# Modulation vectors by multiply-and-sum on VectorE over a transposed matrix, in place of matmuls, copies and transposes

## Chip, cores and metric
The kernel runs on one core of one Trainium2 chip. The metric is the device time of one execution in microseconds (us); shown is the median of three runs. TensorE is called PE, VectorE DVE, ScalarE ACT, GpSimd POOL and SyncE SP, as in the profile. PEld is PE's weight load.

## What is computed
Two residual blocks follow one another over 256 tokens of 1024 channels, each with two layers. In both, each layer first derives a modulation (shift, scale and gate, 1024 numbers each) from a conditioning vector; block 2 does so for the stream x and for a context stream, from two vectors and with the same matrix. Everything is float32.

```python
def hybrid_layer(x, c_silu, ...):                      # block 1, two layers
    mod = c_silu @ w_ada + b_ada                       # [1, 1024] x [1024, 3072]
    shift, scale, gate = jnp.split(mod, 3, axis=-1)
    u = rms_norm(x, norm_g) * (1 + scale[:, None]) + shift[:, None]
    z = u @ w_in
    # three attentions (a: top-k index selection, b: sliding window, c: stick-breaking) on parts of z
    merged = (jax.nn.sigmoid(ma) * (ya @ w_br_a) + jax.nn.sigmoid(mb) * (yb @ w_br_b)
              + jax.nn.sigmoid(mc) * (yc @ w_br_c))
    return x + gate[:, None] * (merged @ w_out)

def mixer_layer(x, cx, c, c_ctx, ...):                 # block 2, two layers
    shift, scale, gate = jnp.split(jax.nn.silu(c) @ w_ada + b_ada, 3, axis=-1)
    shift_c, scale_c, gate_c = jnp.split(jax.nn.silu(c_ctx) @ w_ada + b_ada, 3, axis=-1)
    h = x * (1.0 + scale[:, None]) + shift[:, None]
    hc = cx * (1.0 + scale_c) + shift_c
    # h @ w_in, hc @ w_in, four mixers (A recurrent, B and D attention, C differential attention)
    x_new = layer_norm(alpha * x + gate[:, None] * (y @ w_out), ln_g, ln_b)
```

## The kernel before
The streams are kept channel-major, 128 partitions by 8 channel groups by 256 tokens (`xT`). Every large product is made of three, since each operand is split into a high and a low part: a weight tile of 256 columns arrives as two half tiles of 512 KB (`wr`, issued by SP), ACT copies out the high part `wh` (L111), DVE subtracts for the low part `wl` (L112), and PE runs high by high, low by high and high by low (L104, `proj_tok` and `proj_ch`). There are three `wr` buffers and four each of `wh` and `wl`. The input u of a layer is split likewise: DVE makes `af` (L439), ACT `uh`, DVE `ul` (L441). In block 2 the same tiles are `hxh`, `hxl` for the stream x and `hch`, `hcl` for the context.

A norm (`rstd_row`, L321) sums squares over channels on PE with a matrix of ones, turns them into a column pair `rc` (L329 on DVE, a power on POOL), spreads them with a diagonal `dg` (L333) on PE again and copies the row to `rstd` (L336). Until `af`, `uh` and `ul` of the first channel groups are there, PE has no product of the next layer to run.

The modulation is made by jobs (`ada`, L271). A job makes 256 of the 3072 numbers: it loads two half tiles of w_ada (into `wsp`, which takes idle tags, or into `wr`), runs 8 products with the 32 columns `cs` of conditioning vectors as the small operand (L288; the trace counts two instructions each), copies the sum to `adas` on ACT (L290), transposes it twice on PE (L293, shown under L108), and ends with a reduction `adar` (L295) and a multiply-and-add `mod` (L296) on DVE. Each layer has 12 jobs in each block, 48 in all; one job serves both of block 2's vectors. Eight run at the start, since the first layer's shift and scale are needed at once. The others wait in a list `bg`; `after_tile` (L235) adds `rate` to `due` behind each weight tile and runs a job for each whole number reached. The rates are 0.32 in block 1's first layer, 0.2 in its second and 0.8 in block 2's first. `flush(4)` behind each layer of block 1 runs what is left but four, and `fill` (L241) runs four of these at the norm between block 1's layers and two at the norm into block 2, with weights in tags that are idle there.

The order in each engine's queue isn't that of the code: the tile framework schedules the program once, by its own estimates of times, and each engine then works through its queue in order. So a waiting instruction holds back all behind it on its engine, on SP's queue of transfers too.

## Time and profile before
| | |
|---|---|
| median of 3 runs | 1383.55 us (1381.17 to 1384.69) |
| profiled execution, span | 1377.4 us |
| time outside the span, against the median | 6.2 us |
| PE busy | 1330.4 us (97%) |
| PEld busy | 1164.2 us (85%) |
| DVE busy | 844.3 us (61%) |
| ACT busy | 655.1 us (48%) |
| POOL busy | 25.4 us (2%) |

The profile was taken from one execution. Its span runs from the first to the last instruction that it shows; the median was taken over other executions and holds 6.2 us more. Busy times of matmuls are those of pipelined instructions, each shown longer than the distance to the next. Durations on DVE overlap a little too where its queue is full: the next instruction starts before the last has ended. Block 1's first layer runs to about 372 us, its second to about 717, block 2's first to about 1088, its second to the end.

### The profile page before, as it was taken

The page shows a single profiled execution, that of the slowest core. Times are in us where ns is not written, and L with a number is a line of the kernel's source. Part 1 is how long each engine was busy: PE and PEld are TensorE (multiplying, and loading weights), DVE is VectorE, ACT ScalarE, POOL GpSimd, SP SyncE. Part 2 cuts the span into 40 slices and gives each one's busy share as a digit, 9 for nine tenths or more (in the row PEclk, how much of TensorE's full clock was granted, in tenths as well). Part 3 has the DMA queues.
Part 4 walks back from the last instruction along what each step waited for, and adds up shares of the span by engine and source line. Part 5 has one row for each costly group of instructions (what it writes and reads, how often), then busy time and mean ns, then how long its engine had stood idle before and what let it go on. Part 6 is the DMA issues. An engine that isn't in the chain of part 4 may idle for free.

```text
span 1377.4 us, 27990 instructions
## 1 busy us (share of the span) xinstructions
PE 1330.4 (97%) x11682; PEld 1164.2 (85%) x11682; DVE 844.3 (61%) x1744; ACT 655.1 (48%) x1178; POOL 25.4 (2%) x23
## 2 busy tenths in 40 slices
PE   5999999999999999999998999999999998999996
PEld 2998987899889898789998989977877788997774
DVE  3795454655559544565576366756577777775764
ACT  3455555544444545654443233346455546534652
POOL 0000000000000000000000000000000000000000
PEclk9899999999999999999999999999999999999998
DMA  9754746568746474547764442322143355522111
GB/s 330 216 151 131 232 142 190 158 204 266 227 124 184 123 212 141 153 138 220 211 214 153 135 142 63 109 93 77 52 139 118 107 154 159 175 81 62 62 62 46
DMA packets 199214, 205.07 MB, mean 149 GB/s; under 512 B 8368, under 2 KB 197424, under 8 KB 198448
## 3 DMA queue, kind: packets, MB, share of 16 engines
q1 hardware_dynamic: 199088, 203.28, 48.3%
q8 instruction: 92, 1.51, 0.4%
q14 instruction: 34, 0.28, 0.1%
HBM read 199.06 MB, written 4.19 MB: 148 GB/s over the span
## 4 chain that ended last, share of the span: by engine, by line
PE 82%; DMA 6%; DVE 4%; issue 4%; ACT 2%; SPq 1%; POOL 0%; POOLq 0%; ACTq 0%; DVEq 0%
PE ps L104 77%; PE ps L108 5%; DMA wr<-w_in 4%; DMA wsp<-w_ada 2%; DVE wl L112 2%; ACT wh L111 1%; SPq L219 1%; DMA wr<-w_out 0%; DMA cT<-ctx 0%; DVE KTc L829 0%; DVE af L439 0%; ACT Xx L1305 0%; ACT pe L402 0%; ACT L566 0%; DVE QTc L827 0%
## 5 line engine op out<-in xcount | busy, mean ns | idle before, releaser
L112 DVE TENSOR_TENSOR wl<-wr,wh 128x1024 fp32r<-128x1024 f32 (+1 forms) x270 | 328.4, 1217 | 258.3 <-ACT wh L111 255.8
L111 ACT ACTIVATE wh<-wr 128x1024 fp32r<-128x1024 f32 (+1 forms) x270 | 284.6, 1055 | 378.2 <-PE ps L104 255.2
L104 PE MATMUL ps<-uh,wh 128*128 128x256 f32 x704 | 202.2, 287 | 2.4 <-ACT thm L566 2.4
L104 PE MATMUL ps<-ul,wh 128*128 128x256 f32 x704 | 200.9, 285 | 0.0
L104 PE MATMUL ps<-uh,wl 128*128 128x256 f32 x704 | 200.8, 285 | 0.0
L104 PEld LDWEIGHTS ps<-uh,wh 128*128 128x128 f32 x704 | 132.7, 188 | 8.2 <-issue 4.4
L104 PEld LDWEIGHTS ps<-ul,wh 128*128 128x128 f32 x704 | 132.8, 189 | 1.9 <-issue 1.7
L104 PEld LDWEIGHTS ps<-uh,wl 128*128 128x128 f32 x704 | 132.7, 188 | 1.9 <-issue 1.6
L104 PE MATMUL ps<-wh,uh 128*128 128x256 f32 (+1 forms) x416 | 120.2, 291 | 2.0 <-ACT uh L440 1.2
L104 PE MATMUL ps<-wl,uh 128*128 128x256 f32 (+1 forms) x416 | 119.9, 289 | 1.0 <-DVE wl L112 1.0
L104 PE MATMUL ps<-wh,ul 128*128 128x256 f32 (+1 forms) x416 | 120.0, 289 | 0.1
L402 ACT ACTIVATE pe<-ps,nm 128x512 f32<-128x512 f32 (+2 forms) x160 | 84.9, 539 | 54.4 <-DVE nm L397 41.1
L397 DVE TENSOR_REDUCE nm<-ps 128x1 f32<-128x512 f32 (+2 forms) x104 | 71.1, 687 | 42.2 <-PE ps L104 42.0
L104 PEld LDWEIGHTS ps<-wh,uh 128*128 128x128 f32 x416 | 81.2, 196 | 4.1 <-ACT uh L440 1.4
L104 PEld LDWEIGHTS ps<-wl,uh 128*128 128x128 f32 x416 | 81.3, 196 | 1.8 <-DVE wl L112 1.3
L104 PEld LDWEIGHTS ps<-wh,ul 128*128 128x128 f32 x416 | 81.5, 196 | 1.2 <-DVE ul L441 0.9
L104 PE MATMUL ps<-wh,hxh 128*128 128x256 f32 x256 | 72.4, 283 | 0.0
L104 PE MATMUL ps<-wh,hxl 128*128 128x256 f32 x256 | 72.1, 281 | 0.0
L104 PE MATMUL ps<-wl,hxh 128*128 128x256 f32 x256 | 72.0, 281 | 0.0
L104 PE MATMUL ps<-hxh,wh 128*128 128x256 f32 x224 | 64.9, 294 | 4.2 <-ACT hxh L440 4.2
L104 PE MATMUL ps<-hxl,wh 128*128 128x256 f32 x224 | 64.6, 290 | 2.7 <-DVE hxl L441 2.7
L104 PE MATMUL ps<-hxh,wl 128*128 128x256 f32 x224 | 64.6, 290 | 0.6 <-DVE wl L112 0.6
(351 smaller groups left out, 3150.7 us busy)
## 6 DMA issues: line engine op xcount, KB each, us to landing
wr<-w_in SPq DMA_DIRECT2D x204, 512.0 KB, 4.0
wsp<-w_ada SPq DMA_DIRECT2D x68, 512.0 KB, 5.7
wr<-w_out SPq DMA_DIRECT2D x40, 512.0 KB, 3.7
wr<-w_ada SPq DMA_DIRECT2D x28, 512.0 KB, 3.9
wr<-w_br_a SPq DMA_DIRECT2D x8, 512.0 KB, 3.9
wr<-w_br_c SPq DMA_DIRECT2D x8, 512.0 KB, 4.6
wr<-w_br_b SPq DMA_DIRECT2D x8, 512.0 KB, 4.6
Xx<-resx SPq DMA_DIRECT2D x2, 1024.0 KB, 4.7
```

Of the source, the lines that this page charges most:

```text
L104: self.nc.tensor.matmul(o, l, r, start=start, stop=stop, skip_group_check=True)
L108: self.nc.tensor.transpose(o, i, self.ident[:n, :n])
L111: self.nc.scalar.activation(h, x, AF.Copy)
L112: self.nc.vector.tensor_tensor(l, x, h, op=OP.subtract)
L219: self.nc.sync.dma_start(out=w[:, :, :n], in_=ap[k0 * 128:k0 * 128 + 512, c0:c0 + n].rearrange("(k p) n -> p k n", p=128))
L397: nc.vector.tensor_reduce(nmx, p, axis=AX.X, op=OP.max, negate=True)
L402: nc.scalar.activation(e[:, j, :], p[:, j, :], AF.Exp, bias=nm[:, h:h + 1], accum_out=ss[:, h:h + 1])
```

## The change
The two matrices w_ada and w_ada_2 are handed over transposed, so that a chunk holds 128 outputs on the partitions and the 1024 inputs along a row of 4 KB. A conditioning vector is loaded once onto all 128 partitions (`cond_row`), and twice its silu is made in place (tanh on ACT, one multiply-and-add on DVE, in two halves). A job is now two chunks; for each and for each vector, one DVE instruction multiplies chunk and vector, sums along the row, halves, adds the bias and leaves a column of `mod`. The products themselves go to `junk`, a single bfloat16 buffer that nobody reads. In the program it is two entries on DVE, the sum and the read of its accumulator: 144 pairs. The column operand `cs`, the copies and the transposes go, and both `fill` with them; the rates are 0.5, 0.3 and 0.8. A setting makes the framework's scratch space for transfers smaller, which frees on-chip memory for the new buffers. On PE the program has 8070 rows before and 7964 now, on DVE 1399 and 1604, on ACT 755 and 707, on SP 153 and 162.

```diff
-    def fill(self, n, tags):
-        """waiting jobs for a stretch in which the streams' chain leaves TensorE idle; their weights go to idle tags"""
-        keep, self.spare = self.spare, tags
-        for _ in range(min(n, len(self.bg))):
-            self.bg.popleft()()
-        self.spare = keep
...
+    def cond_row(self, v):
+        nc = self.nc
+        r = self.const.tile([128, 1024], F32, name="crow", tag=f"crow{v // 2}")
+        src = self.I["cond"][1024 * v:1024 * v + 1024]
+        nc.sync.dma_start(out=r, in_=bass.AP(tensor=src.tensor, offset=src.offset, ap=[[0, 128], [1, 1024]]))
+        for h in (slice(0, 512), slice(512, 1024)):
+            th = self.W("cth", [128, 512], tag="th")
+            nc.scalar.activation(th, r[:, h], AF.Tanh, scale=0.5)
+            nc.vector.scalar_tensor_tensor(r[:, h], th, 1.0, r[:, h], op0=OP.add, op1=OP.mult)
+        return r
...
         def load(n):
-            return [self.raw(wa, k, n * 256, 256, True) for k in (0, 4)]
+            ws = []
+            for c in (2 * n, 2 * n + 1):
+                if self.spare:
+                    w = self.K("wsp", [128, 1024], tag=self.spare[self.nspare % len(self.spare)])
+                    self.nspare += 1
+                else:
+                    w = self.wr.tile([128, 1024], F32, name="wr", tag="wr")
+                nc.sync.dma_start(out=w, in_=wa[:, c])
+                ws.append(w)
+            return ws
 
         def job(n, ws=None):
-            p = self.P(self.pj, [128, 512])
-            for k in range(8):
-                g = 32 * (k % 4)
-                self.mm(p[g:g + 32, :256], self.cs[:, k, :], ws[k // 4][:, k % 4, :], start=k < 4, stop=k >= 4)
-            sb = self.W("adas", [128, 256], tag="score")
-            nc.scalar.activation(sb, p[:, :256], AF.Copy)
-            pc = self.P(self.tr, [128, 2, 4, 32])
-            for j in range(2):
-                self.T(pc[:, j].rearrange("p g v -> p (g v)"), sb[:, 128 * j:128 * j + 128])
-            r = self.W("adar", [128, 2, nv])
-            nc.vector.tensor_reduce(r, pc[:, :, :, v0:v0 + nv].rearrange("p j g v -> p j v g"), axis=AX.X, op=OP.add)
...
+            for c, w in enumerate(ws or load(n)):
+                c += 2 * n
+                for v, r in enumerate(crow):
+                    junk = self.const.tile([128, 1024], BF, name="junk", tag="junk")
+                    nc.vector.tensor_tensor_reduce(out=junk, in0=w, in1=r, scale=0.5, scalar=bias[:, c:c + 1],
+                                                   op0=OP.mult, op1=OP.add, accum_out=mod[:, c, v:v + 1])
...
-        if l == 1:
-            self.fill(4, ["a4", "a5", "a6", "g1", "g2", "g3", "t3a", "t3b"])
...
-        N.rate = 0.32 if l == 0 else 0.2
+        N.rate = 0.5 if l == 0 else 0.3
...
-    N.fill(2, ["a7", "g1", "g2", "g3"])
...
+    for n in ("w_ada", "w_ada_2"):
+        a[n] = np.ascontiguousarray(inputs[n].reshape(2, 1024, 24, 128).transpose(0, 3, 2, 1))
+    a["cond"] = np.concatenate([inputs[n].reshape(-1) for n in ("c", "c_2", "c_ctx_2")])
```

The queue of DVE at the start, where the first layer's input is made. The names: `g1` and `mod10` come from the modulation, `rstd` from the norm, `c_identb` is a constant. Before:

```order
L449 SCALAR_TENSOR_TENSOR g1_322<-mod10_106,cols_87 128x2
L439 SCALAR_TENSOR_TENSOR af_353<-xT_117,g1_322,rstd_320 128x256
L439 SCALAR_TENSOR_TENSOR af_357<-xT_117,g1_322,rstd_320 128x256
L112 TENSOR_TENSOR wl_364<-wr_279,wh_363 128x1024
L441 SCALAR_TENSOR_TENSOR ul_328<-af_353,mod10_106,uh_327 128x256
L112 TENSOR_TENSOR wl_368<-wr_281,wh_367 128x1024
L441 SCALAR_TENSOR_TENSOR ul_328<-af_357,mod10_106,uh_327 128x256
L112 TENSOR_TENSOR wl_434<-pre_283,wh_433 128x1024
L112 TENSOR_TENSOR wl_438<-pre_283,wh_437 128x1024
L167 CAST c_identb_577<-cb_571 128x128
```

And now, the last parts of the same input:

```order
L112 TENSOR_TENSOR wl_261<-wr_176,wh_260 128x1024
L440 SCALAR_TENSOR_TENSOR ul_225<-af_242,mod10_107,uh_224 128x256
L440 SCALAR_TENSOR_TENSOR ul_225<-af_246,mod10_107,uh_224 128x256
L296 ISA junk_174,mod10_107<-wsp_170,crow_99,cols_87 128x1024
L296 ISA mod10_107 128x1
L112 TENSOR_TENSOR wl_265<-wr_178,wh_264 128x1024
L112 TENSOR_TENSOR wl_331<-pre_180,wh_330 128x1024
L448 SCALAR_TENSOR_TENSOR g1_219<-mod10_107,cols_87 128x2
L112 TENSOR_TENSOR wl_335<-pre_180,wh_334 128x1024
L438 SCALAR_TENSOR_TENSOR af_250<-xT_118,g1_219,rstd_217 128x256
L438 SCALAR_TENSOR_TENSOR af_254<-xT_118,g1_219,rstd_217 128x256
L158 CAST c_identb_474<-cb_468 128x128
```

The sums stand where the small reductions stood, and the last `ul` moved to a place further down than the rows shown, behind four `wl` and behind constants that wait for transfers (`csg`, `pr`).

The queue of DVE at the norm between block 1's two layers. Before:

```order
L336 COPY rstd_4206<-ps_4196 128x256
L295 TENSOR_REDUCE adar_4328<-ps_4325 128x2
L439 SCALAR_TENSOR_TENSOR af_4215<-xT_117,g1_4208,rstd_4206 128x256
L439 SCALAR_TENSOR_TENSOR af_4219<-xT_117,g1_4208,rstd_4206 128x256
L296 SCALAR_TENSOR_TENSOR mod11_290<-adar_4328,cols_87 128x2
L581 TENSOR_SCALAR g4_7749<-mod11_290 128x8
L441 SCALAR_TENSOR_TENSOR ul_4214<-af_4215,mod11_290,uh_4213 128x256
L441 SCALAR_TENSOR_TENSOR ul_4214<-af_4219,mod11_290,uh_4213 128x256
L439 SCALAR_TENSOR_TENSOR af_4223<-xT_117,g1_4208,rstd_4206 128x256
L439 SCALAR_TENSOR_TENSOR af_4227<-xT_117,g1_4208,rstd_4206 128x256
L441 SCALAR_TENSOR_TENSOR ul_4214<-af_4223,mod11_290,uh_4213 128x256
L441 SCALAR_TENSOR_TENSOR ul_4214<-af_4227,mod11_290,uh_4213 128x256
```

And now (`mod20_3965` is the modulation of block 2's first layer, `crow_3949` and `crow_3957` its two vectors; `mod11` is that of the layer whose input is made):

```order
L335 COPY rstd_3995<-ps_3985 128x256
L296 ISA junk_5471,mod20_3965<-wsp_5463,crow_3957,cols_87 128x1024
L296 ISA mod20_3965 128x1
L438 SCALAR_TENSOR_TENSOR af_4004<-xT_118,g1_3997,rstd_3995 128x256
L438 SCALAR_TENSOR_TENSOR af_4008<-xT_118,g1_3997,rstd_3995 128x256
L296 ISA junk_5800,mod20_3965<-wsp_5796,crow_3949,cols_87 128x1024
L296 ISA mod20_3965 128x1
L703 COPY mc_7712<-mod20_3965 128x8
L703 COPY mc_7792<-mod20_3965 128x8
L440 SCALAR_TENSOR_TENSOR ul_4003<-af_4004,mod11_187,uh_4002 128x256
```

Sums for the block behind the next layer moved in between the steps that make u.

SP's queue of transfers at the same place, among the second layer's first weights (the rows with 68 columns are the narrow tile of the index weights). Before:

```order
L219 DMA wr_4413<-w_in 128x4x256
L219 DMA wr_4479<-w_in 128x4x68
L219 DMA wsp_4310<-w_ada 128x4x256
L219 DMA wr_4485<-w_in 128x4x68
L219 DMA wsp_4312<-w_ada 128x4x256
L219 DMA wr_4635<-w_in 128x4x256
L219 DMA wsp_4976<-w_ada_2 128x4x256
L219 DMA wsp_4978<-w_ada_2 128x4x256
L219 DMA wr_4641<-w_in 128x4x256
```

And now:

```order
L210 DMA wr_4190<-w_in 128x4x68
L210 DMA wr_4340<-w_in 128x4x256
L287 DMA wsp_5463<-w_ada_2 128x1024
L287 DMA wsp_5796<-w_ada_2 128x1024
L287 DMA wsp_5798<-w_ada_2 128x1024
L287 DMA wsp_6273<-w_ada_2 128x1024
L287 DMA wsp_6275<-w_ada_2 128x1024
L287 DMA wsp_6471<-w_ada_2 128x1024
L287 DMA wsp_6473<-w_ada_2 128x1024
L287 DMA wsp_6674<-w_ada_2 128x1024
L210 DMA wr_4346<-w_in 128x4x256
```

Eight chunks moved into one row ahead of the next weights; they use two tags, `t3a` and `t3b`.

## Rows read from the trace of the kernel before
**Rows 1.** The page: busy times of the engines, and the ended-last chain by line.
```profile
PE 1330.4 (97%) x11682; PEld 1164.2 (85%) x11682; DVE 844.3 (61%) x1744; ACT 655.1 (48%) x1178; POOL 25.4 (2%) x23
PE ps L104 77%; PE ps L108 5%; DMA wr<-w_in 4%; DMA wsp<-w_ada 2%; DVE wl L112 2%; ACT wh L111 1%; SPq L219 1%; DMA wr<-w_out 0%; DMA cT<-ctx 0%; DVE KTc L829 0%; DVE af L439 0%; ACT Xx L1305 0%; ACT pe L402 0%; ACT L566 0%; DVE QTc L827 0%
```
**Rows 2.** Windows: stretch, length, busy time (instructions) by engine, granted clock, DMA share, GB/s.
```profile
34.00:97.00 63.00, 61.73 (x482) 59.92 (x483) 51.35 (x127) 29.59 (x53) 0.00 (x0) 0.92 0.64 191
372.80:433.80 61.00, 58.09 (x481) 52.35 (x472) 42.17 (x100) 25.41 (x41) 0.70 (x1) 0.94 0.53 151
732.00:1088.00 356.00, 351.13 (x3482) 299.19 (x3482) 218.17 (x513) 155.19 (x332) 13.26 (x9) 1.00 0.34 105
```
**Rows 3.** Windows of `cs` alone (one row: PE, PEld, ACT), then of `adas`.
```profile
732.00:1088.00 356.00, 17.82 (x214) 6.62 (x214) 0.00 (x0) 0.75 (x2) 1.00 0.34 105
...
34.00:365.00 331.00, 3.87 (x20) 2.39 (x20) 3.80 (x10) 0.98 0.63 189
365.00:384.00 19.00, 2.57 (x12) 1.24 (x12) 2.29 (x6) 1.00 0.76 237
384.00:717.00 333.00, 3.10 (x16) 1.94 (x16) 3.03 (x8) 0.99 0.57 172
717.00:732.00 15.00, 0.85 (x4) 0.49 (x4) 1.02 (x3) 0.96 0.43 137
732.00:1088.00 356.00, 5.46 (x28) 3.40 (x28) 5.04 (x14) 1.00 0.34 105
```
**Rows 4.** Timeline of PE: start, duration, engine, line, operation, out<-in, shapes, count.
```profile
437.38 1.07 PE L104 MATMUL ps<-wsp,cs 128*32 128x256 f32 x16
438.38 0.60 PE L104 MATMUL ps<-akT,aqT 64*128 64x128 f32 x3
...
156.81 0.39 PE L108 MATMUL ps<-ident,adas 128*128 128x128 f32 x2
156.95 0.36 PE L104 MATMUL ps<-uh,wl 128*128 128x256 f32 x1
```
**Rows 5.** Groups of DVE by form: busy us, mean ns, idle before and releasers.
```profile
L112 DVE TENSOR_TENSOR wl<-wr,wh 128x1024 fp32r<-128x1024 f32 x268 | 327.6, 1223 | 255.6 <-ACT wh L111 253.2 <-ACT pe L402 0.8 <-PE ps L104 0.2
L933 DVE SCALAR_TENSOR_TENSOR pe<-pe,dc 128x512 f32<-128x512 f32 x16 | 12.0, 750 | 0.5
L439 DVE SCALAR_TENSOR_TENSOR af<-xT,g,rstd 128x256 f32<-128x256 f32 x16 | 7.0, 478 | 0.1
L608 DVE RECIPROCAL rec<-ss 128x1 f32<-128x1 f32 x32 | 5.1, 159 | 5.9 <-ACT pe L402 5.6
```
**Rows 6.** Timeline of DVE at the start, where the first input is finished.
```profile
34.80 1.22 DVE L112 TENSOR_TENSOR wl<-wr,wh 128x1024 fp32r<-128x1024 f32 x1
35.94 0.47 DVE L441 SCALAR_TENSOR_TENSOR ul<-af,mod,uh 128x256 fp32r<-128x256 f32 x1
...
37.47 0.47 DVE L441 SCALAR_TENSOR_TENSOR ul<-af,mod,uh 128x256 fp32r<-128x256 f32 x1
```
**Rows 7.** Windows of the start: the columns as in rows 2.
```profile
8.00:12.00 4.00, 3.10 (x22) 0.69 (x18) 0.33 (x2) 0.65 (x2) 0.00 (x0) 1.00 1.04 397
12.00:34.00 22.00, 15.13 (x132) 6.05 (x132) 8.64 (x34) 8.59 (x19) 0.70 (x1) 0.93 1.10 349
```
**Rows 8.** The ended-last chain in order of time, at the norm: start, us, what.
```profile
372.92 6.08 DMA wsp<-w_ada
```
**Rows 9.** Timeline of DVE at the same norm and behind it.
```profile
371.96 0.87 DVE L587 SCALAR_TENSOR_TENSOR xT<-ps,g,xT 128x256 f32<-128x256 f32 x2
...
388.74 0.88 DVE L441 SCALAR_TENSOR_TENSOR ul<-af,mod,uh 128x256 fp32r<-128x256 f32 x2 [0.18 <-ACT uh L440]
...
431.01 1.23 DVE L112 TENSOR_TENSOR wl<-wr,wh 128x1024 fp32r<-128x1024 f32 x1 [0.19 <-ACT wh L111]
```
**Rows 10.** The page, DMA issues: count, KB each, median us from issue to landing.
```profile
wsp<-w_ada SPq DMA_DIRECT2D x68, 512.0 KB, 5.7
```
**Rows 11.** Timeline of PE at the norm into block 2; idle before in brackets.
```profile
729.87 0.38 PE L104 MATMUL ps<-hxh,wh 128*128 128x256 f32 x1 [3.99 <-ACT hxh L440]
```

More of the change, by code (lines that the diff above doesn't have):

```diff
@@ L122, in load_consts @@
         self.mhalf = C.tile([128, 8], F32, name="mhalf")
-        self.cs = C.tile([128, 8, 32], F32, name="cs")
-        nc.vector.memset(self.cs, 0.0)
-        th = self.W("cth", [128, 24], tag="af")
-        nc.scalar.activation(th, cols[:, :24], AF.Tanh, scale=0.5)
-        for j in range(3):
-            o = 8 * j
-            nc.vector.scalar_tensor_tensor(self.cs[:, :, j], th[:, o:o + 8], 1.0, cols[:, o:o + 8],
-                                           op0=OP.add, op1=OP.mult)
         nc.vector.memset(self.sel4, 0.0)
@@ L271, in ada @@
     def ada(self, l, blk):
         nc = self.nc
-        nv = 1 if blk == 1 else 2
+        vs = (0,) if blk == 1 else (1, 2)
         wa = self.I["w_ada" if blk == 1 else "w_ada_2"][l]
-        v0 = blk - 1
-        mod = self.const.tile([128, 24, nv], F32, name=f"mod{blk}{l}")
-        def load(n):
-            return [self.raw(wa, k, n * 256, 256, True) for k in (0, 4)]
-        def job(n, ws=None):
-            ws = ws or load(n)
-            bias = self.colB[:, 48 * (blk - 1) + 24 * l:48 * (blk - 1) + 24 * l + 24]
-            p = self.P(self.pj, [128, 512])
-            for k in range(8):
-                g = 32 * (k % 4)
-                self.mm(p[g:g + 32, :256], self.cs[:, k, :], ws[k // 4][:, k % 4, :], start=k < 4, stop=k >= 4)
-            sb = self.W("adas", [128, 256], tag="score")
-            nc.scalar.activation(sb, p[:, :256], AF.Copy)
-            pc = self.P(self.tr, [128, 2, 4, 32])
-            for j in range(2):
-                self.T(pc[:, j].rearrange("p g v -> p (g v)"), sb[:, 128 * j:128 * j + 128])
-            r = self.W("adar", [128, 2, nv])
-            nc.vector.tensor_reduce(r, pc[:, :, :, v0:v0 + nv].rearrange("p j g v -> p j v g"), axis=AX.X, op=OP.add)
-            nc.vector.scalar_tensor_tensor(mod[:, 2 * n:2 * n + 2, :], r, 0.5,
-                                           bias[:, 2 * n:2 * n + 2][:, :, None].to_broadcast([128, 2, nv]),
-                                           op0=OP.mult, op1=OP.add)
@@ new lines, in ada @@
+        if l == 0:
+            self.crow = [self.cond_row(v) for v in vs]
+        crow = self.crow
+        mod = self.const.tile([128, 24, len(vs)], F32, name=f"mod{blk}{l}")
+        bias = self.colB[:, 48 * (blk - 1) + 24 * l:48 * (blk - 1) + 24 * l + 24]
+        def load(n):
+            ws = []
[8 more added lines that the diff above has]
+            return ws
@@ L1319, in _arrays @@
     a["cols"] = np.ascontiguousarray(np.concatenate(
-        [col(n) for n in ("c", "c_2", "c_ctx_2", "b_ada", "b_ada_2", "final_g", "norm_g", "ln_g_2", "ln_b_2")]
+        [col(n) for n in ("b_ada", "b_ada_2", "final_g", "norm_g", "ln_g_2", "ln_b_2")]
         + [twice(n) for n in ("hg_norm_g_2", "df_subln_g_2")] + [col("hg_lb_logits_2")], 1))
+    for n in ("w_ada", "w_ada_2"):
+        a[n] = np.ascontiguousarray(inputs[n].reshape(2, 1024, 24, 128).transpose(0, 3, 2, 1))
+    a["cond"] = np.concatenate([inputs[n].reshape(-1) for n in ("c", "c_2", "c_ctx_2")])
     a["rows"] = np.concatenate([inputs[n].reshape(-1) for n in (
```

6 lines of the change are left out of this document (3 added, 3 removed).

## Prediction
> **What bounds the kernel now.** I read the page's busy times first, then the chain that ended last, then the stretches one by one. TensorE (PE) is busy 1330.4 us of a span of 1377.4, and its products are 77% of the chain; VectorE (DVE) is busy 844.3 us, 61% [rows 1]. So the kernel is bound by PE almost everywhere, and a us that leaves PE's queue in a PE-bound stretch is a us off the end, as long as DVE still delivers the low weight halves `wl` in time. That average hides the places where DVE is already nearly full: 51.4 us of the 63 us behind the first product, and 42.2 of the 61 us behind the norm between block 1's two layers, while in block 2's first layer it has 138 us free of 356 [rows 2]. The change takes work from the engine that sets the end and gives about three times as much to DVE, so the question is where DVE has the room.
>
> **What leaves PE.** A job is 8 products (16 instructions) over `cs` and two transposes of `adas`. By the transposes, two to a job, there are 10 jobs from 34 to 365 us, 6 in the norm's gap, 8 from 384 to 717, 2 at the norm into block 2 and 14 behind it [rows 3]; the other 8 of the 48 are done in the first 34 us. Those 8 lie under the loading of the weights, the 6 lie in a gap in which PE has nothing else. That leaves 34 jobs on PE-bound stretches. One costs from start to start 1.00 us for the products and 0.14 for the transposes [rows 4], so 1.14 at the least; by busy time it is 17.82 / 14 + 5.46 / 14 = 1.66 with the overlap of pipelined ends counted in [rows 3]. I take 1.3, nearer to the start-to-start value: 34 x 1.3 = **-44 us** (-39 to -56). The ACT copy and DVE's two small operations of a job go too; they lie beside PE and bring nothing of their own.
>
> **What DVE gets.** There are 144 new multiply-and-sum instructions over 128 x 1024 (24 + 24 for block 1's two layers, 48 + 48 for block 2's, since there each chunk meets two vectors). The trace has none. From below: the subtraction that makes `wl`, 1024 elements from two SBUF inputs, takes 1223 ns, 1.14 from its start to the next instruction's when the queue is full [rows 5, 6]. From above: multiply-and-scale of 512 elements takes 750 ns, two of them 1.50, and a one-column operation behind it 159 ns, together 1.66 [rows 5]. I take 1.14 + 0.16 for the read of the sum + 0.1 for the wait on the one before (all write one `junk` buffer) = **1.4 us**; 144 x 1.4 = 202 us, which would put DVE near 1020 us of busy time. That still is under the span, so what matters is where they stand in DVE's queue, which works in order.
>
> [...]
>
> **The start (+5).** Before, weights land without a pause: 349 GB/s at a DMA share of 1.10, and 397 GB/s in the four us in which `xT`, with long rows, lands [rows 7]. The transposed matrix has rows of 4 KB instead of 1 KB, so its 8.4 MB could come in 21 us instead of 24; the broadcast vector of 0.5 MB costs 1.3 of it. Against that, 16 sums (22.4 us) now stand in DVE's queue between the steps that make the input u, where small reductions stood, and they can't begin before the vector's tanh. Behind the last chunk DVE still has to make parts of u, four `wl` and the constants; in the new order the last two `ul` stand behind constants that wait for transfers. Adding the rows in order puts the last `ul` near 44 to 45 us; before it stood at 37.47 [rows 6]. The first tile's products need it; they still had work of their own in hand at 37.47, so I take +5 of the 7 (0 to 10). In the 63 us behind it, DVE gets 16 sums; with the constants moved ahead the order adds up to 62.1 us against 62.5 elapsed, so DVE is full but not late: 0 (to +4).
>
> **The norm between block 1's layers (+17).** Before, the gap is stretched by the filled-in jobs themselves: a load of w_ada of 6.08 us stands on the chain there, and PE's queue holds the norm's sums behind its products [rows 8]. From the last `xT` (start 371.96) the last `ul` starts at 388.74; the `wl` of the twelfth full weight half behind it is made from 431.01 [rows 9], when PE is about to need it. The fill's removal shortens the gap by up to 4 us. But in the new order 17 sums of the next block's vectors stand from the last `xT` to the first narrow `wl`, in ones between each two pairs of `af` and `ul`, then four in a row: DVE was the idle engine there, so the scheduler put them there. The sum over DVE's queue from `xT` to that twelfth half is now 29 x 1.4 = 40.6 for the sums and 32.7 for the rest (the 42.2 of [rows 2] without overlaps and without the top-k selection, which now stands later), 73.3 in place of 60: PE is late by 13, the fill's removal counted in, since the sum begins at `xT`. By the same sum DVE has caught up some 108 us behind `xT`. On top, eight loads of chunks stand in SP's queue in one row and go to two buffers: a chunk can be fetched only when the sums over the last but one are done, and a load takes 5.7 us to land [rows 10] while DVE has 4.5 us of other work for each chunk. That gives 0 to 1.2 us for each of eight; I add 4 (0 to 9). Together **+17** (9 to 24). Who waits: `rc`, `dg`, `rstd` and `af` stand behind sums in the same queue, ACT's `uh` behind `af`, PE behind both; the weights of the next tiles wait in SP's queue behind the eight loads.
>
> **The norm into block 2 (+4).** PE's gap there is 3.99 us [rows 11], part filled by jobs. Sums now stand between `rc`, `dg`, `rstd` and `af`; about three of them at 1.4 us fall into the chain: +4 (2 to 6).
>
> **Block 2's first layer (+7).** 48 sums, 67 us, go into 138 us of free DVE time, and PE is ahead by the saved jobs. A stall comes where an operation that PE waits for finds a sum at work: 67 of 356 us are taken, a half sum (0.7 us) is left on average, and there are some 48 row maxima there: 48 x 0.19 x 0.7 = 6.4. I take +7 (3 to 18). Block 2's second layer has no jobs: 0.
>
> **The sum.** -44 + 5 + 0 + 17 + 4 + 7 = -11, so the span goes from 1377.4 to 1366. The median of the runs, 1383.55, stands 6.2 above the profiled span; with that, **1372**. The ends: -56 + 0 + 0 + 9 + 2 + 3 = -42 gives 1342, -39 + 10 + 4 + 24 + 6 + 18 = +23 gives 1407; all at one end at once is unlikely, and I take 1347 to 1403 for it.
>
> **Rivals.** A: DVE's room hides it all, because a sum is as cheap as `wl` and the order leaves the chain ahead. For it: 533 us of idle DVE time in all. Against it: the norm's queue, where even 1.14 a sum leaves 29 x 1.14 + 32.7 = 65.8 against 60. With -44, or -48 with the fill gone, it gives 1383.6 - 48 = **1336**.
> [...]
> C, the slower side: in block 2's first layer the softmax chains are one after another through DVE and ACT to PE, so a sum that stands ahead of a row maximum is not taken at random but put just where DVE is idle, which is where PE waits for it. If half of the 67 us is exposed, 34 instead of 7, the time is 1372 + 27 = **1399**. It turns slower than before from 7 + 12 = 19 us exposed, about 3 in 10 of the sums' time. For it: the same scheduler put sums into each gap of the norm. Against it: PE is 351 of 356 us busy there [rows 2], so it has little to wait for and tiles enough in hand.
> That the jobs don't leave PE can't be: the program's order has 106 instruction rows fewer on PE and no `adas`.
>
> **Chances.** Forecast 0.6, A 0.12, B 0.08, C 0.2. About 0.3% (4 us) is what a measurement can tell from no change: faster is under 1379.4, slower over 1387.7. Of the forecast's 0.6 I give 0.44 to faster, 0.09 to the same and 0.07 to slower; A is faster; B is slower; C is 0.03 same and 0.17 slower. Faster 0.56, same 0.12, slower 0.32. The range, which leaves out A below and B above (0.2 together) and takes in C, is 1346 to 1404.
>
> **What would show it.** PE's busy time should fall by some 75 us over the whole span and its idle time rise. [...] The last `ul` should start about 44 us at the start, and 27 us behind the last `xT` at the norm instead of 17. DVE should be busy 1000 to 1040 us, and PE's waits for `wl` and `ul` should be some 20 us longer. From 384 to 1088 no more than 7 us should be waits of PE for row maxima behind sums; over 20 means C. What would make me wrong most is the price of one sum: each 0.1 us moves the start and the norm by 3 to 6 us together.

## The result, and the profile after
The changed kernel takes 1395.62 us (median of four runs, 1390.64 to 1400.41) against 1382.36 for the kernel before (median of four, one run more than above): ratio 1.0095, interval 1.0066 to 1.0124. It is 13 us slower where 11 us faster was forecast. The profiled execution has a span of 1392.3 us (1377.4 before).

First the page of the changed kernel, the lines that answer to [rows 1], and the two groups of the new sums (busy us, mean ns of one, idle time before them and what ended it):

```profile
PE 1281.8 (92%) x10818; PEld 1147.5 (82%) x10818; DVE 1000.1 (72%) x1938; ACT 648.5 (47%) x1140; POOL 31.0 (2%) x23
PE ps L104 27%; DMA wr<-w_ada 4%; PE ps L108 3%; DVE junk L296 2%; DVE wl L112 1%; DVE nm L396 0%; POOL rec L347 0%; ACT wh L111 0%; DVE KTc L826 0%; ACT Xx L1301 0%; DVE Gx L428 0%; ACT pe L401 0%; DVE QTc L824 0%; DVE FTc L829 0%; DVE ssq L877 0%
...
L296 DVE CUSTOM_DVE_ANT_0 junk<-wsp,crow,cols 128x1024 bf16<-128x1024 f32 x96 | 123.0, 1281 | 12.8 <-DMA wsp<-w_ada 12.4
...
L296 DVE CUSTOM_DVE_ANT_0 junk<-wr,crow,cols 128x1024 bf16<-128x1024 f32 x48 | 61.6, 1283 | 29.6 <-DMA wr<-w_ada 29.0
```

PE lost 49 us of busy time and the span grew by 15: PE is idle 64 us more than before. DVE gained 156 us, less than the 202 of the forecast: a sum takes 1.28 us, 16 us of small operations are gone, and busy time counts the overlapped ends of back-to-back instructions once (DVE's groups add up to 1095 us here and 910 before, its busy time is 1000 and 844). New on the chain is `wr<-w_ada`: a load that only jobs wait for. (The chain could be followed back only to 753 us here, so its shares are not to be compared with those of before.) And DVE itself sits idle 41 us in front of sums whose chunk has not landed.

The windows (stretch, length, then busy time of PE, PEld, DVE, ACT and POOL, granted clock, DMA share, GB/s) show where DVE is full, first of the changed kernel, then two of the same stretches before:

```profile
31.00:165.00 134.00, 123.58 (x1005) 119.12 (x1006) 124.50 (x242) 58.07 (x86) 0.00 (x0) 0.99 0.94 308
379.00:440.00 61.00, 47.97 (x302) 43.67 (x303) 57.11 (x104) 17.17 (x28) 1.66 (x1) 0.72 0.66 196
735.00:935.00 200.00, 178.93 (x2129) 170.86 (x2130) 161.68 (x316) 63.73 (x108) 11.44 (x6) 0.96 0.43 129
...
379.00:440.00 61.00, 59.06 (x464) 54.85 (x465) 45.51 (x103) 26.11 (x39) 0.08 (x1) 0.94 0.50 142
735.00:935.00 200.00, 198.59 (x2347) 178.44 (x2347) 113.80 (x246) 71.84 (x132) 8.87 (x6) 1.00 0.36 111
```

DVE is busy 93% from the first product to 165 us; 94% in the norm between block 1's layers and behind it, where PE is busy 48 of 61 us and the granted clock is 0.72 (as a share of the highest; of the first 1365 windows of 1 us of this trace 1264 show 1.00 and 77 show 0.50); and 81% in the first 200 us of block 2. To these 161.7 us come the waits for chunks there, in the list of DVE's waits from 735 to 935 us (who waited for whom: us in total, times, longest):

```profile
DVE junk L296 <- DMA wr<-w_ada: 27.9, 17, 3.8
```

161.7 + 27.9 is 189.6 of 200 us: all but full. Then the sums' places over the span, 40 slices of 34.8 us, in tenths busy:

```profile
busy tenths in 40 slices 5233100000453300000012323210000000000000
```

They stand in three bunches: the start to 155 us, 353 to 476 us (across the norm between block 1's layers), 722 to 933 us. Between them DVE has no sum for 198 and 246 us. The rates of the jobs don't show in these places; the account for that is that the scheduler takes a job as soon as a buffer for its chunk is free (e12 below bears it out).

### The profile page after: what moved, and what is told of

The parts are those of the page before. It is cut to its first block, busy times and chain, and to the rows that moved or that the text cites. A ratio compares the mean times of both kernels' runs of the same rounds, so it can differ in the third digit from the quotient of the medians.

```text
span 1392.3 us, 26487 instructions
## 1 busy us (share of the span) xinstructions
PE 1281.8 (92%) x10818; PEld 1147.5 (82%) x10818; DVE 1000.1 (72%) x1938; ACT 648.5 (47%) x1140; POOL 31.0 (2%) x23
## 5 line engine op out<-in xcount | busy, mean ns | idle before, releaser
L104 PE MATMUL ps<-wh,uh 128*128 128x256 f32 (+1 forms) x416 | 123.9, 300 | 18.4 <-ACT wh L111 8.0
L296 DVE CUSTOM_DVE_ANT_0 junk<-wsp,crow,cols 128x1024 bf16<-128x1024 f32 x96 | 123.0, 1281 | 12.8 <-DMA wsp<-w_ada 12.4
L104 PE MATMUL ps<-wh,ul 128*128 128x256 f32 (+1 forms) x416 | 124.0, 299 | 3.8 <-DVE ul L440 3.8
L104 PEld LDWEIGHTS ps<-wh,uh 128*128 128x128 f32 x416 | 84.2, 204 | 22.1 <-ACT wh L111 8.7
L104 PEld LDWEIGHTS ps<-wh,ul 128*128 128x128 f32 x416 | 84.5, 203 | 6.7 <-DVE ul L440 5.4
L104 PEld LDWEIGHTS ps<-wl,uh 128*128 128x128 f32 x416 | 84.2, 203 | 5.4 <-DVE wl L112 5.0
L296 DVE CUSTOM_DVE_ANT_0 junk<-wr,crow,cols 128x1024 bf16<-128x1024 f32 x48 | 61.6, 1283 | 29.6 <-DMA wr<-w_ada 29.0
```

The lines of the kernel that those rows point to most:

```text
L104: self.nc.tensor.matmul(o, l, r, start=start, stop=stop, skip_group_check=True)
L296: nc.vector.tensor_tensor_reduce(out=junk, in0=w, in1=r, scale=0.5, scalar=bias[:, c:c + 1], op0=OP.mult, op1=OP.add, accum_out=mod[:, c, ...
```

## The experiments
All runs in one table: the span, and the stages of the profiled execution, in us. "Layer 1" ends with the last update of `xT` (counted from 0, the start included); a norm ends with the first product that uses the new input's low part (`ul`), or the first on `hxh` for block 2; block 2's first layer ends with the last gated update of the stream, `Xx<-ps,g,Xx`. What follows takes 265 to 268 us in every run. Stages with the same order of instructions differ by up to 3 us from run to run. More can come from the order alone: an edit elsewhere makes the scheduler place the first layer's instructions differently too, and in e1, whose edit is in block 2, that layer took 5.7 us longer.

| run | layer 1 | norm | layer 2 | norm | block 2, layer 1 | span |
|---|---|---|---|---|---|---|
| before | 372.8 | 10.9 | 333.5 | 12.7 | 381.0 | 1377.4 |
| changed | 379.3 | 14.0 | 332.6 | 13.7 | 387.4 | 1392.3 |
| e1 own buffers, block 2 | 385.0 | 12.4 | 332.9 | 9.9 | 383.7 | 1390.8 |
| e2 one chunk, block 2 | 380.4 | 13.8 | 343.6 | 11.9 | 368.6 | 1385.8 |
| e3 half sums, block 2 | 381.4 | 13.6 | 330.2 | 13.0 | 363.9 | 1367.7 |
| e4 no jobs | 351.4 | 7.5 | 326.9 | 9.9 | 363.7 | 1324.5 |
| e5 block 1 spread | 365.7 | 7.6 | 330.4 | 16.5 | 386.1 | 1372.3 |
| e6 layer 2 spread | 377.2 | 7.5 | 329.4 | 16.2 | 388.5 | 1384.0 |
| e7 four `wr` | 387.9 | 12.3 | 331.0 | 13.4 | 382.2 | 1392.3 |
| e8 all sums half | 371.6 | 10.1 | 335.8 | 13.8 | 371.0 | 1367.2 |
| e9 block 2's sums early, some | 368.8 | 12.0 | 358.2 | 17.2 | 359.8 | 1380.7 |
| e10 the same, all | 368.0 | 11.0 | 370.1 | 8.9 | 365.3 | 1389.0 |
| e11 before, new schedule | 387.1 | 7.5 | 340.4 | 11.0 | 386.0 | 1398.0 |
| e12 changed, old schedule | 373.0 | 13.2 | 338.4 | 14.8 | 386.3 | 1391.0 |
| e13 spread further | 384.4 | 8.7 | 331.0 | 18.0 | 366.0 | 1375.4 |
| e14 spread further yet | 385.1 | 10.6 | 333.6 | 17.8 | 361.7 | 1373.6 |
| e15 before, no fills | 375.4 | 7.4 | 332.3 | 32.5 | 391.0 | 1406.2 |
| e16 e14 with late vectors | 376.6 | 12.3 | 339.4 | 18.3 | 361.3 | 1373.4 |
| e17 e16 with fewer moved | 376.5 | 8.3 | 333.9 | 28.3 | 358.2 | 1370.4 |

### Block 2: buffers, loads, or the sums' own time (e1 to e4, e7)
Two theories on block 2 stood first: that chunks lack buffers, or that the sums' time in the queue costs.

e1, with tag g2 idle in block 2:

```diff
-    N.spare = None
+    N.spare = ["g2", "cw"]
     x, r = N.block2(0, R, H, mod, context_done)
```

> The changed kernel, but in block 2 the 24 chunks of w_ada go to two buffers of their own instead of the three `wr` buffers of the weights. Stage meant: block 2's first layer, 739.5 to 1126.9 us in the changed kernel (387.4 us, before 381.0). Theory T (buffer loop): a sum waits at the head of DVE's queue for a chunk whose load could start only when sums before it had freed a `wr` buffer, and the weights' splits wait behind it; then DVE's waits for w_ada fall from 29.0 us to under 10, the stage to 366-374 us, the run to about 1378. Rival W (work and order): the 48 sums' 65 us in an in-order queue do it, wherever the chunks lie; then the stage stays at 384-391 and the run within 5 us of 1395.

1394.08 us, ratio 1.0098 (1.0068 to 1.0128). Theory T's condition came, waits for chunks of 1.6 us in the stage, but not its time; the run is where rival W has it, the stage (383.7) at the edge of W's range. A clean test it isn't: the scheduler used the buffers to move 20 sums up into block 1 and 28 down to the layer's end. Windows of e1, columns as above:

```profile
740.00:850.00 110.00, 109.76 (x1258) 107.16 (x1259) 67.55 (x136) 37.29 (x58) 5.29 (x4) 0.98 0.29 87
850.00:950.00 100.00, 100.00 (x1107) 84.86 (x1105) 59.73 (x130) 44.65 (x98) 3.27 (x2) 1.00 0.18 54
950.00:1040.00 90.00, 86.55 (x626) 74.77 (x626) 62.58 (x140) 48.05 (x113) 1.64 (x1) 1.00 0.22 67
1040.00:1100.00 60.00, 47.95 (x264) 28.63 (x263) 57.77 (x142) 22.78 (x51) 4.33 (x2) 0.74 0.45 138
```

With no sums from 740 to 950, PE has next to no gap; from 1040 to 1100, with 25 of the 28 among the last softmaxes and the context's norm, DVE is at 96% and PE at 48 of 60 us and a granted clock of 0.74. So the loss moved with the sums.

e2 and e3, in block 2's first layer only: all sums over one chunk that stays on the chip, with the other 23 loads left out (the first two parts of the diff), and sums over half the columns (the last part):

```diff
+        if blk == 2 and l == 1:
+            one = self.K("wsp", [128, 1024], tag="g2")
+            nc.sync.dma_start(out=one, in_=wa[:, 0])
...
+            if blk == 2 and l == 1:
+                return [one, one]
             ws = []
...
+                    q = 512 if blk == 2 and l == 1 else 1024
-                    nc.vector.tensor_tensor_reduce(out=junk, in0=w, in1=r, scale=0.5, scalar=bias[:, c:c + 1],
+                    nc.vector.tensor_tensor_reduce(out=junk[:, :q], in0=w[:, :q], in1=r[:, :q], scale=0.5, scalar=bias[:, c:c + 1],
```

> The changed kernel, but block 2's second modulation (48 sums in its first layer) is summed from one chunk that is loaded once; the other 23 loads are left out, so these numbers of the modulation are not the reference's. All of the sums stay. Theory T: without waiting for chunks the stage (387.4 us in the changed kernel) falls to 362-372 us. Rival W: all of DVE's work is still there, so 382-390.

> The changed kernel, but the 48 sums of block 2's first layer run over 512 of the 1024 columns (half of each sum is left out), with all chunks loaded as before. A sum should take about 0.7 us instead of 1.28. Theory T: the loop of buffer, load (3.7 us) and sums stays and each turn is 1.2 us shorter: the stage 379-386 us. Rival W: half of DVE's 65 us goes, and with it half of what the stage has over PE's own need (about 360 us): 368-376.

e2: 1383.26 us. The stage is 368.6, but some 30 of the sums, now free of loads, went up into block 1's second layer, which grew by 11: theory T's number, not its proof. e3: 1374.45 us, ratio 0.9961 (0.9940 to 0.9982), with the waits for chunks little changed: 22.3 us in the stage's first 200. The sums' group in e3, with its waits over the whole run (count, then duration ns: least, median, most), and then the windows of block 2's first 200 us, of e3 and of e4:

```profile
L297 DVE CUSTOM_DVE_ANT_0 junk<-wr,crow,cols x48: 742/751/756, 721.3 to 931.6; 128x512 bf16<-128x512 f32 x48
...
  DMA wr<-w_ada: 23.8, 17
```

```profile
738.00:938.00 200.00, 195.67 (x2257) 182.44 (x2258) 143.84 (x326) 72.61 (x130) 10.18 (x6) 0.99 0.41 125
```

```profile
696.00:896.00 200.00, 200.00 (x2286) 184.63 (x2286) 119.96 (x248) 75.05 (x136) 8.56 (x6) 0.99 0.24 72
```

48 x 0.53 = 25.5 us less in DVE's queue made the stage 23.5 us shorter, down to that without jobs. Without jobs DVE has 80 us free in those 200. The sums that stand in them, alone (busy time of DVE and count, then clock and DMA), in the changed kernel, in e3 and in e7, which follows below:

```profile
735.00:935.00 200.00, 55.18 (x43) 0.96 0.43 129
738.00:938.00 200.00, 30.00 (x40) 0.99 0.41 125
745.00:945.00 200.00, 49.27 (x39) 0.94 0.41 125
```

With their waits whole sums need 55 + 28 = 83 us, half sums 30 + 22 = 52, and PE stands idle 21 and 4 us there. That fits a queue that has room for 80 us, but it is an account of few runs, not a law. Rival W was nearer, though it expected half of this.

e4 sets the vectors to the bias and leaves out every job:

```diff
+        for v in range(len(vs)):
+            nc.vector.tensor_copy(mod[:, :, v], bias)
+        return mod, [lambda ws=None: None for n in range(12)], lambda n: None
```

> The changed kernel without any modulation job: the vectors are set to the bias, no chunk is loaded and no sum runs. It gives each stage's time without the jobs. If one job costs PE 1.3 us, then against the kernel before: block 1's second layer 333.5 - 8 x 1.3 = 323 us, block 2's first layer 381.0 - 14 x 1.3 = 363 us, block 1's first layer 338.6 - 10 x 1.3 = 326 us, the start shorter by some 20 us since 8 MB need not land first; about 1310 us in all. If the stages stay within 4 us of before, the jobs' matmuls were hidden, and there was nothing for the change to gain.

1325.79 us. Against it, before spends 10.0 us on block 1's second layer with its norm and 20.0 on block 2's first with its norm: there the price of 1.3 a job holds (10.4 and 20.8). In the first layer, counted from its first product (34.2 us before, 20.6 here), it spends only 7.8 us where 13 were due, since PE then waits 4.2 us for ACT's `thm`, a gap that the jobs' products had filled (1.2 before). The start gave back 14 us instead of 20; so the run is longer than expected. Behind the first product, then, all jobs together were worth some 38 us, not the forecast's 44.

e7 is the plain test of buffers: `pool("wr", 4)`.

> The changed kernel with four `wr` buffers instead of three, for weights and chunks alike. If DVE's waits for chunks in block 2 (29.0 us) come from too few buffers and are what costs there, they fall to under 15 us and the stage from the norm into block 2 to the end of its first layer (401 us in the changed kernel, 374 without jobs) to 385-392. If the sums' own time in the queue is what costs, as the run with half sums suggests, the stage stays at 396-402.

1395.20 us: the waits for chunks in block 2 fell to 13.2 us, the stage with its norm only from 401.1 to 395.6, just under the range that was given for no effect of buffers, and the first layer, in another order, lost 9. Buffers are not the main thing. By the count above the sums need 49 + 13 = 62 of 80 us, and PE's idle time from 745 to 945 us did fall to 8. What didn't come back is the clock. Norm and stage as one window, of the changed kernel, e3, e4 and e7:

```profile
725.80:1126.90 401.10, 372.63 (x3489) 325.43 (x3488) 293.76 (x625) 167.18 (x341) 16.53 (x10) 0.95 0.33 101
725.20:1102.00 376.80, 362.43 (x3486) 318.06 (x3485) 269.71 (x622) 166.89 (x341) 15.31 (x10) 0.99 0.35 107
685.80:1059.50 373.70, 365.12 (x3489) 320.99 (x3488) 238.84 (x529) 164.73 (x339) 14.90 (x10) 0.99 0.25 75
731.20:1126.80 395.60, 375.52 (x3481) 326.11 (x3480) 292.46 (x624) 166.19 (x340) 16.71 (x10) 0.94 0.33 101
```

PE has the same products in all four. From the changed kernel to e3 its idle time falls by 14.1 us and its busy time by 10.2, as the granted clock rises from 0.95 to 0.99. So the 24 us of e3 are not DVE's 25.5 handed on one for one. In e7 the idle time falls by 8.4, but the clock doesn't rise and the busy time grows by 2.9. Why the clock stays low there is open.

### Block 1: place or time (e5, e6, e8)
e5 holds a chunk's load behind the weights of the tile whose job it belongs to (`behind` tells the scheduler to issue it after them), sets the rates to 0.42 and 0.32, and lets the second layer's jobs begin later; e6 holds the loads back in the second layer alone, with the change's rates. The diff is that of e5:

```diff
-        self.nc.sync.dma_start(out=w[:, :, :n], in_=ap[k0 * 128:k0 * 128 + 512, c0:c0 + n].rearrange(
...
+            self.lastw = self.nc.sync.dma_start(out=w[:, :, :n], in_=ap[k0 * 128:k0 * 128 + 512, c0:c0 + n].rearrange(
...
-                nc.sync.dma_start(out=w, in_=wa[:, c])
+                with self.behind(self.lastw if blk == 2 and l == 0 or blk == 1 and l == 1 and n < 6 else None):
+                    self.lastc = nc.sync.dma_start(out=w, in_=wa[:, c])
...
-        N.rate = 0.5 if l == 0 else 0.3
-        N.due = -2.0 if l == 0 else 0.0
+        N.rate = 0.42 if l == 0 else 0.32
+        N.due = -2.0 if l == 0 else -2.0
```

> The changed kernel with block 1's sums spread out: in SP's queue a chunk's load may not stand ahead of the weights of the tile whose job it belongs to (second modulation of block 1 up to its sixth job, first of block 2), the rates are 0.42 and 0.32, and the second layer's jobs begin four tiles later. Every sum and load stays; no sum stands in DVE's queue at the norm between the layers any more. Theory P (place): a bunch of sums, with DVE's waits for their chunks, fills DVE's in-order queue and PE starves; spread out they fit into DVE's idle time. Then the end of the first layer comes at 366-373 us instead of 379, the norm takes 8-10 us instead of 14, the second layer 328-333 instead of 333 us, and the run is about 1376. Rival W (work): 48 sums cost block 1's layers the same wherever they stand; then every stage stays within 4 us of the changed kernel and the run at 1391-1398.

> The same for the second layer of block 1 alone, with the change's own rates: only the loads of block 2's first modulation are held behind their tile's weights. Theory P: norm and second layer of block 1 together 346.5 us in the changed kernel, then 336-341 (334 without any job), the first layer as in the changed kernel (379 +-3). Rival W: 344-349.

e5: 1376.31 us, ratio 0.9975 (0.9960 to 0.9991) to before: theory P, and the first complete kernel here that beats both. e6: 1385.95 us, 336.9 for norm and layer instead of 346.6, as theory P has it. The sums' places in e5, and its windows of block 1's second part:

```profile
busy tenths in 40 slices 5300001031000022112331322110200000000000
```

```profile
366.00:440.00 74.00, 69.80 (x528) 65.65 (x529) 55.80 (x129) 32.86 (x60) 0.70 (x1) 0.91 0.47 131
440.00:704.00 264.00, 255.91 (x2033) 238.28 (x2033) 192.55 (x308) 138.47 (x216) 0.00 (x0) 0.99 0.59 187
```

No sum stands in the norm's slices; in the layer DVE is at 73%. The 42 sums that stand in the second layer and its norm then cost 3.6 us (338.0 against 334.4 without jobs).

e8 halves all sums, as e3 did in block 2.

> The changed kernel with all 144 sums over 512 of 1024 columns (half of each sum is left out), all loads as before. DVE's time for sums falls from 196 to about 120 us. If DVE's time in its queue is the cost in block 1 as it was in block 2: the end of the first layer 368-372 us instead of 379, the norm with the second layer 339-342 instead of 346.5, the run near 1350. If block 1's loss comes from the order alone (the products' and selection's places, not the sums' time), the first layer ends at 376-380.

1369.39 us, not near 1350. The first layer came down by 7.7 to 371.6, as expected; norm and second layer only by 0.7 in sum, not by 4 to 7, and why is not shown. Place (e5) did more for block 1 than halving the work where it stood.

### The schedule (e11, e12, e15)
The change also drops the jobs at the norms and raises the rates. e11 does that to the kernel before, e15 only drops the jobs, e12 gives the changed kernel the old rates and fills.

```diff
-        if l == 1:
-            self.fill(4, ["a4", "a5", "a6", "g1", "g2", "g3", "t3a", "t3b"])
...
-        N.rate = 0.32 if l == 0 else 0.2
+        N.rate = 0.5 if l == 0 else 0.3
...
-    N.fill(2, ["a7", "g1", "g2", "g3"])
```

> The kernel before, with its matmul jobs, but with the change's rates (0.5 and 0.3) and without the jobs that were run at the two norms. It tells the schedule's share of the change from that of the sums. If the schedule itself costs, the norm between block 1's layers stays at 11 us or more and the run is at 1388 or more; if the jobs at the norms only lengthened them, the norm falls to 7-9 us, the jobs cost PE 6 x 1.3 us elsewhere, and the run is within 4 us of before (1377-1385).

> The kernel before without the jobs run at the norms, rates as they were (0.32, 0.2): which part of the changed schedule cost 19 us with matmul jobs. If it is the rates, this run is at 1378-1386, and the norm between block 1's layers takes 7-9 us instead of 10.9. If it is the missing fills, it is at 1392 or more.

> The changed kernel with the schedule of before: rates 0.32 and 0.2, and the jobs run at the two norms. The run with matmul jobs and the changed schedule took 1400 us, 19 more than before. If the schedule's price adds to that of the sums, this run is 15-20 us faster than the changed kernel, 1375-1381. If the scheduler hoists the sums to wherever a buffer is free, whatever the rates say (in the program, the first layer's sums stand as in the changed kernel, up to the 30th weight half), it stays at 1389-1398, with the norm between block 1's layers at 12 us or more.

e11: 1400.22 us, e15: 1405.27, e12: 1392.75 (ratio 1.0075, 1.0047 to 1.0103). With matmul jobs the new schedule costs 19 us. Without the fills alone, at the old rates (e15), it is 24, most of it where the leftovers pile up: 20 us at the norm into block 2 and 10 in the layer behind it. At the new rates (e11) these jobs stand in block 1's layers, which grow by 14 and 7 us. The sums hardly feel the schedule: e12 stays within 3 us of the changed kernel. Under one and the same new schedule sums beat matmuls by 5 us (1395.62 against 1400.22), but that is the median of two runs, and the intervals of the two ratios overlap; the old kernel's schedule was the better one for its jobs.

### Moving block 2's sums (e9, e10, e13, e14, e16)
e9 and e10 hold every load behind its tile's weights and queue block 2's second modulation in block 1's second layer already, at a rate of 0.55 (six jobs left for block 2) and 0.65 (none).

> As the run with block 1's sums spread out, and half of the jobs of block 2's second modulation moved up: all jobs of both of block 2's modulations are queued in block 1's second layer at a rate of 0.55, and six of the 24 jobs of that layer are left for block 2. Theory P (place): DVE has 128 us free in that layer and sums that stand behind their tile's weights cost little; so block 2's first layer with its norm, 402.6 us in the run with block 1's sums spread, falls to 382-390, the second layer of block 1 with its norm (338.0) grows by 3-7, and the run comes to 1360-1368 us. Rival W: the 24 sums cost where they go what they cost where they were; the run stays at 1373-1380.

> The same with a rate of 0.65 and none left: all 96 sums of block 2 stand in block 1's second layer (about 130 us on DVE, which has 128 us free there before the change). Theory P: block 2's first layer with its norm falls to 374-379 us (374 without any job), the second layer of block 1 gets too full and grows by 10-25; the run 1355-1368 us. Rival W: 1373-1380.

e9: 1383.36 us; e10: 1396.55, both above every range that was given. Block 2's first layer came down to that without jobs, as theory P said, but block 1's second grew by 28 and 40 against e5. The window of e9's second layer shows why: DVE at 82% over the whole layer, PE at a clock of 0.94.

```profile
381.00:739.00 358.00, 332.89 (x2536) 310.92 (x2535) 294.54 (x510) 171.13 (x269) 0.00 (x0) 0.94 0.62 196
```

So place isn't all: 42 sums in that layer and its norm cost 4 us, 88 cost 36 (370.2 against 334.4 for norm and layer). e13 and e14 therefore spread all sums over all three layers, and e16 does it with the vectors of block 2 loaded late.

> All sums held behind their tile's weights, and spread evenly: five jobs of block 2's first modulation moved up to block 1's first layer, five of its second to block 1's second layer, seven left for block 2 at a rate of 0.45; each of the three vectors has its own buffer. By place alone: block 1's first layer ends at 367-371 us (365.7 with block 1's sums spread and none moved), norm and second layer as there (338 +-3), norm into block 2 and its first layer fall from 402.6 to 387-394; 1362-1370 us. If a sum costs DVE's queue the same wherever it goes, 1373-1380.

> The same with eight jobs of block 2's first modulation in block 1's first layer, eight of its second in block 1's second, four left for block 2. By place alone 1358-1368 us, with block 2's first layer and its norm at 380-388 and the first layer of block 1 ending at 369-375. If the cost of a sum grows with the share of DVE that is taken (as in the second layer when it held 88 sums), it is no better than the run before: 1366-1376.

> As the run with four jobs left for block 2, but the vectors of block 2 are loaded and put through tanh only when the first of its jobs is due. In that run their tanh stood ahead of the first norm's squares, in the same buffers, and the first product came at 49.9 us instead of 31. By place alone: first product back at 31 us, first layer's end at 366-372 (385.1 there), the rest as there; 1355-1363 us, about 1.6% faster than before. If the start's loss comes back later, 1370-1377.

e13: 1377.56 us, e14: 1374.93, both in the range of the second alternative; e16: 1370.37, ratio to before 0.9922 (0.9906 to 0.9939), the fastest complete kernel of this case. In e13 and e14 the tanh of block 2's vectors stood ahead of the first norm's squares and the first product came at 50 us; e16 mends that (31.5 us), but of the 18 us only 8.5 are left at the first layer's end: place alone would have given 1355 to 1363, so the second alternative (1370 to 1377) holds here too. A last run, e17, was to move three jobs fewer up into the first layer and one fewer into the second. It took 1373.78, within 5 us of e16 as expected if place is all. Its first layer ends where that of e16 does, but holds only two sums fewer (55 for 57), so it doesn't tell whether e16's was too full.

## Why the prediction was wrong
**Right.** The price of a job (1.3 us) in block 1's second layer and in block 2, though not in the first layer (e4), and that of a sum: 1.28 us and 0.08 for the read, where 1.4 was taken. DVE's busy time came out at the lower end of its 1000 to 1040 us. PE's busy time fell by 49 us, not by 75, and its waits for `wl` and `ul` grew by some 8 us, not 20: PE stood elsewhere. The two places worked out from the order came out nearly to the digit; the timeline of DVE in the changed kernel, at the start and at the norm:

```profile
44.34 0.49 DVE L440 SCALAR_TENSOR_TENSOR ul<-af,mod,uh 128x256 fp32r<-128x256 f32 x1
...
378.41 0.87 DVE L584 SCALAR_TENSOR_TENSOR xT<-ps,g,xT 128x256 f32<-128x256 f32 x2
...
404.68 0.88 DVE L440 SCALAR_TENSOR_TENSOR ul<-af,mod,uh 128x256 fp32r<-128x256 f32 x2
```

The last `ul` starts at 44.3 us (44 to 45 forecast) and 26.3 us behind `xT` (27 forecast). The norm with block 1's second layer came out 2.2 us over before, where -10 + 17 = +7 was forecast; without the bunch (e6) they are 9.7 us shorter, so its price was 10 rather than 17. The sum takes 1283 ns for 1024 columns and 751 for 512 (e3), 1.04 ns an element, the rate of the two-input operations without a sum (1.06: 478 ns for 256 columns, 750 for 512 [rows 5]). Rival B, to which the chances give 0.08, was a sum at half that rate; no run shows one.

**Wrong: "DVE is full but not late: 0 (to +4)"**, the first layer behind its start. The layer ended 6.5 us after that of before, where -13 + 5 = -8 was due: 14.5 us off. The step compared the sum of durations with the time elapsed over 63 us, stopped there, and took a queue that is full to be one that is on time. For those 63 us PE bears it out: it has no gap from 44.9 to 158.6 us, at a granted clock of 1.00. But the sums go on to 155 us at the same pace, 35 of them from 31 us on, and DVE falls behind with work that PE needs only later. Two windows of the changed kernel, then the maxima of the top-k selection in the first layer (count, duration ns, first and last start), in the changed kernel and before:

```profile
44.90:158.60 113.70, 113.70 (x956) 110.46 (x956) 104.27 (x196) 51.30 (x77) 0.00 (x0) 1.00 0.93 301
158.60:246.00 87.40, 74.22 (x500) 63.33 (x500) 42.31 (x72) 54.51 (x84) 0.00 (x0) 0.94 0.38 112
...
L500 DVE MAX8 m<-score x16: 283/357/428, 88.2 to 165.8; 128x8 f32<-128x128 f32 x8, 128x8 f32<-128x256 f32 x8
L503 DVE MAX8 m<-score x16: 285/356/430, 68.7 to 103.1; 128x8 f32<-128x128 f32 x8, 128x8 f32<-128x256 f32 x8
```

The selection ends at 166 us instead of 103, and PE stands 13 us of the 87 behind 158.6, with no sum in DVE's queue any more. PE's waits in the changed kernel from 36 to 372 us; before, that list has 1.2 us for `thm` and 1.0 for `wl`, and nothing else:

```profile
PE ps L104 <- ACT thm L563: 6.0, 2, 4.8
PE ps L104 <- DVE rt L369: 5.2, 1, 5.2
PE ps L104 <- DVE wl L112: 4.7, 2, 4.1
```

The gap of 5.2 us begins at 158.7 us: PE waits for a result's buffer that `rt` frees, and `rt` stood behind two `wl` and steps of the late selection; the first `wl` waited 2.0 us itself. The gap at `rt` is 3.6 to 5.8 us in every run with 35 sums between 31 and 165 us (the changed kernel, e1, e2, e3, e6, e7), 0.5 in e12 with 27, and gone with half sums (e8) or 12 (e5). So the bunch makes it. Of the 14.5 us, some 13 are the sums' and 5 the jobs' smaller worth (the wait for `thm`, e4); the start gave about 4 back, since it cost some 1 us and not 5 (first product 3.2 us earlier, then 5.1 us of gaps to 44 us where before had 1.0). With the sums spread out (e5) the layer ends at 365.7 us, 7.1 before that of before. That is near the forecast's -8, but by other terms: the errors at the start and in the jobs' price cancel there.

**Wrong: "+7 (3 to 18)" for block 2's first layer.** With its norm it came out 7.4 us longer than before instead of 10 shorter; over e4 the sums cost 27 us there, where 4 + 7 were forecast. Two things were mis-sized. The term spread 48 sums over 356 us; the scheduler put them into 200. And it counted a sum's 1.4 us, but not the time that the sum stands at the head of the queue with its chunk still on the way: 27.9 us. On the chain of the changed kernel this reads (start, us, what):

```profile
785.86 3.74 DMA wr<-w_ada
789.74 1.29 DVE junk L296
791.07 1.28 DVE junk L296
792.39 3.64 DMA wr<-w_ada
796.05 1.29 DVE junk L296
```

Two sums free a buffer, the next chunk's load takes 3.7 us, the next sums wait for it with the weights' splits (`wl`) behind them. Such a wait was priced at the norm (+4) and left out here. Rival C named the place and the point of decision (19 us exposed), and the outcome is on its side. Its mechanism, sums in front of row maxima, isn't shown for the change: by its own sign PE's waits behind row maxima should exceed 20 us, and from 735 to 1125 us PE waits 5.9 us for the `pe` that follow them. In e1, with sums at the layer's end, it waits 10.8.

**Left out: PE's clock.** No term had it. At the norm PE has only the norm's small sums from 376 us on, with gaps of 3.0, 3.4 and 5.1 us between them; at 381.4 us the granted clock falls from 1.00 to 0.50 and stays there until 408.7, 17 us into the next layer's products, which start 0.21 us apart until then and 0.12 from 408.8 on:

```profile
381.40:408.70 27.30, 15.99 (x60) 13.12 (x60) 25.33 (x53) 3.63 (x8) 1.66 (x1) 0.50 0.50 141
```

Before, with jobs in that gap, PE is busy 24.3 of the 27.2 us behind 372.8 at a clock of 0.99; in e6, without the bunch, the clock is low for 10.2 us there. Norm and second layer as one window, of the changed kernel and of e6:

```profile
379.30:725.80 346.50, 331.20 (x2556) 307.64 (x2557) 250.62 (x445) 169.72 (x277) 1.66 (x1) 0.95 0.57 169
377.20:714.20 337.00, 325.12 (x2552) 303.09 (x2552) 258.34 (x454) 171.09 (x275) 0.70 (x1) 0.97 0.58 182
```

For the same products PE is busy 6.1 us longer and idle 3.4 us longer; taking the longer busy time for the clock's part, most of the bunch's price at the norm is clock. In block 2's first layer with its norm it is 7.5 of the 27 us over e4, and 20 are idle time. In the first layer PE's busy time is that of e4 (323.8 us from 31 to 379.3, 323.6 in e4 from 20 to 351, at clocks of 0.99 and 0.98): there the loss is idle time alone.

**Left out: the schedule.** New rates and no fills were taken as harmless once the jobs left PE. In time that was right for the sums (e12), for matmul jobs it is not (e11).

## What to carry to other kernels
Work handed to an engine with idle time on average is free only where that engine is idle, and an instruction that waits for its own data holds its in-order queue as if it ran (27.9 us in 200 here): add its wait to its duration, and compare both with the free time of the stretch it stands in, not of the stage. Follow such a stretch to its end and look behind it: a late queue came due here more than 100 us after the first product, when the sums were over. And work taken out of a gap can leave the engine idle there and its clock low behind it, as here in the first layer (idle: 4.2 us at `thm` in e4, 1.2 before) and at the norm (0.50 for 27.3 us). A scheduler that takes background jobs as soon as a buffer is free bunches them; tying each job's load behind the tile that it should accompany turned a loss of 1% into a gain of 0.3% here, and spreading further into one of 0.8%. Before a change of engine and schedule together, run the new schedule with the old work.

## What the hardware showed unexpectedly
A multiply with a running sum over two float32 inputs took DVE 1.28 us here for 128 x 1024, and its sum was read in 0.08 us by an instruction of its own, less than the 0.16 us of a one-column operation [rows 5].
